# Row sums of squared differences: the first load of x split, another tail, and the tile context closed behind the work

## The chip, the cores and the metric

The kernel runs on one core of a Trainium2 chip. The core has a matrix engine (TensorE or PE, not used here), a vector engine (VectorE or DVE), a scalar engine (ScalarE or ACT), GpSimd (POOL) and SyncE (SP), which here only issues transfers. Sixteen DMA engines carry data between the chip's memory (HBM) and the core's own memory of 128 partitions. The metric is the device time of one execution in microseconds (us); lower is better. Before the change the median of three runs is 85.35 us (85.3 to 85.4).

## The reference

Two arrays of 1024 x 4096 float32 numbers; for each row the sum of the squares of the differences:

```python
def reference(x, y, axis):        # axis = -1
    return np.sum((x - y) ** 2, axis=axis).astype(np.float32)
```

Input is 2 x 16.8 MB, output 4 KB.

## The kernel before

Row 8p + r of the input lies on partition p, so a partition holds eight whole rows side by side: 32768 columns of x and as many of y (N in the code). The text calls the group of 128 rows that share an r "row r"; row r covers the columns 4096 r to 4096 (r + 1). A column of one operand is 128 numbers, 512 bytes. In memory each partition's share is one run of 128 KB.

The core's memory holds six rows of each operand (`X` and `Y`, H = 24576 columns). Columns from 24576 on, rows 6 and 7, go into the places of rows 0 and 1 once these are squared.

**Loads.** The lists `xw` and `yw` give the widths of the pieces, all issued by SyncE on one queue in the order of need (`load`, line 106). Widths shrink towards the end, from 16384 columns to 160. The last 160 columns of row 3 (`late`) are left out of their place in y and loaded after everything else; the last 288 columns of row 7 (`last`) come just before them. A transfer sends one packet for each partition, eight on each of the 16 DMA engines, with as many bytes as the piece has in a partition.

**Work.** For each piece of y VectorE waits for its semaphore and for those of x that it needs (`wait_loaded`, line 153), and subtracts in place, cut at row ends (`sub`, line 163). ScalarE waits for the subtraction and squares with a running sum into one number per partition (`square`, line 168). Where a row has one piece, this number is its result; where it has several, they go into `parts`, and VectorE adds them up (`complete`, line 176): row 6 after the piece with j = 4, row 7 after the last piece. The last piece (row 3's end) isn't given to ScalarE: one VectorE instruction squares, sums, and adds row 3's first part (line 199).

**Order.** There is no scheduler. Each engine's instructions run in the order of the code, and semaphores tie the engines together (`diffs`, `acts`, `sums`, `stored`, one for each load). After the square of row 1 SyncE issues all loads of rows 6 and 7 (line 215). When `sums` is complete it issues the store (line 226).

**Start and end.** The framework puts an entry block in front: all engines pass a barrier there. `Program.early` moves the two first loads (of x and of y) ahead of SyncE's part in it. A `TileContext`, when it is closed, adds a drain, two more barriers of all engines with a clearing of its semaphores between them (there are none to clear where it holds none), and a branch to its block. The kernel closes it at once (line 18), so these barriers stand at the start. The work follows, and at the end GpSimd waits for the store and clears the kernel's semaphores (line 45 and 46).

Of the kernel before, what the change touches and what calls it, by code (L numbers as in the profile page):

```python
# [8 lines left out]
class Program:  # L9
# [4 lines left out]


    def __init__(self, nc, tc):
        self.nc = nc
        tc.close()
        tc.compile()  # L19
        self.here = nc.cur_bb.bb.instructions  # L20
        self.entry = nc.main_func.blocks[0].instructions
        self.before = len(self.here)
        self.sems = []

    def semaphore(self, name):
        self.sems.append(self.nc.alloc_semaphore(name))
        return self.sems[-1]

    def early(self, engine):

        taken = self.here[self.before :]
        del self.here[self.before :]
        where = next(
            n
            for n, i in enumerate(self.entry)
            if i.engine == engine and str(i.opcode) == "Drain"
        )
        self.entry[where:where] = taken

    def close(self, sem, value):  # L40

        self.nc.gpsimd.wait_ge(sem, value)
        self.nc.clear_and_free_semaphores(self.sems)


def kernel(tc, x, y, axis, out):
    nc = tc.nc  # L50
    P = nc.NUM_PARTITIONS
    F32 = mybir.dt.float32
    Square = mybir.ActivationFunctionType.Square
    mult, add = mybir.AluOpType.mult, mybir.AluOpType.add

    B, D = x.shape
    R = B // P
    N = R * D


    xv = x.rearrange("(p r) d -> p (r d)", p=P)
    yv = y.rearrange("(p r) d -> p (r d)", p=P)
    ov = out.rearrange("(p r) -> p r", p=P)


    H = 6 * D
    X = nc.alloc_sbuf_tensor("X", [P, H], F32).ap()
    Y = nc.alloc_sbuf_tensor("Y", [P, H], F32).ap()
    results = nc.alloc_sbuf_tensor("results", [P, R], F32).ap()

    xw = [16384, 8192, 5568, 1824, 512, 288]
    yw = [16224, 8192, 2656, 2912, 928, 896, 512]
    late, last = 160, 288
    LATE = 3
    cut = (LATE + 1) * D - late
    assert sum(xw) == N and sum(yw) == N - late - last
    xs, c = [], 0
    for w in xw:  # L80
        xs.append((c, c + w))
        c += w
    ys, c = [], 0
    for w in yw:
        ys.append((c, c + w))
        c += w
        if c == cut:
            c += late
    ys += [(N - last, N), (cut, cut + late)]

    prog = Program(nc, tc)
    diffs = prog.semaphore("diffs")
    acts = prog.semaphore("acts")
    sums = prog.semaphore("sums")
    stored = prog.semaphore("stored")
    n = dict(diffs=0, acts=0, sums=0)

    def home(c0, c1):
        h0 = c0 % H
        return slice(h0, h0 + c1 - c0)  # L100


    landed_x, landed_y = [], []
    freed = []

    def load(landed, src, dst, name, c0, c1):
        sem = prog.semaphore("%s%d" % (name, len(landed)))
        nc.sync.dma_start(out=dst[:, home(c0, c1)], in_=src[:, c0:c1]).then_inc(sem, 16)  # L108
        landed.append(((c0, c1), sem))

    order = []
    have = 0
    for c0, c1 in ys:
        while have < c1:
            order.append((landed_x, xv, X, "x") + xs[len([o for o in order if o[3] == "x"])])
            have = order[-1][5]
        order.append((landed_y, yv, Y, "y", c0, c1))

    todo = list(order)
    for _ in range(2):  # L120
        load(*todo.pop(0))
    prog.early(mybir.EngineType.SP)
    while todo and todo[0][5] <= H:
        load(*todo.pop(0))


    row_parts = [[] for _ in range(R)]
    for c0, c1 in ys:
        while c0 < c1:
            e = min(c1, (c0 // D + 1) * D)  # L130
            row_parts[c0 // D].append((c0, e))
            c0 = e
    parts, where = None, {}
    total = sum(len(p) for p in row_parts if len(p) > 1)
    parts = nc.alloc_sbuf_tensor("parts", [P, total], F32).ap()
    k = 0
    for r, p in enumerate(row_parts):
        for piece in p:
            where[piece] = parts[:, k : k + 1] if len(p) > 1 else results[:, r : r + 1]
            k += len(p) > 1  # L140
    first = {}
    k = 0
    for r, p in enumerate(row_parts):
        if len(p) > 1:
            first[r] = k
            k += len(p)

    def parts_of(r, m):
        return parts[:, first[r] : first[r] + m]

    seen_x = [0]

    def wait_loaded(c1, ysem):

        waits = []
        while seen_x[0] < len(xs) and xs[seen_x[0]][0] < c1:
            waits.append(seen_x[0])
            seen_x[0] += 1
        nc.vector.wait_ge(ysem, 16)
        for k in waits:  # L160
            nc.vector.wait_ge(landed_x[k][1], 16)

    def sub(c0, c1):
        a = X[:, home(c0, c1)]
        nc.vector.tensor_sub(out=a, in0=a, in1=Y[:, home(c0, c1)]).then_inc(diffs, 1)  # L165
        n["diffs"] += 1

    def square(c0, c1, acc):
        a = X[:, home(c0, c1)]
        nc.scalar.wait_ge(diffs, n["diffs"])  # L170
        nc.scalar.activation(out=a, in_=a, func=Square, accum_out=acc).then_inc(acts, 1)  # L171
        n["acts"] += 1

    squared = {}

    def complete(r):
        nc.vector.wait_ge(acts, squared[row_parts[r][-1]])
        nc.vector.tensor_reduce(  # L178
            out=results[:, r : r + 1],
            in_=parts_of(r, len(row_parts[r])),  # L180
            axis=mybir.AxisListType.X,
            op=add,
        ).then_inc(sums, 1)
        n["sums"] += 1

    for j, (c0, c1) in enumerate(ys):
        final = j == len(ys) - 1
        wait_loaded(c1, landed_y[j][1])
        pieces = []
        while c0 < c1:  # L190
            e = min(c1, (c0 // D + 1) * D)
            pieces.append((c0, e))
            c0 = e
        for piece in pieces:
            sub(*piece)
            r = piece[0] // D
            if final:
                nc.vector.wait_ge(diffs, n["diffs"])
                nc.vector.tensor_tensor_reduce(  # L199
                    out=Y[:, home(*piece)],  # L200
                    in0=X[:, home(*piece)],
                    in1=X[:, home(*piece)],
                    scale=1.0,
                    scalar=parts_of(r, 1),
                    op0=mult,
                    op1=add,
                    accum_out=results[:, r : r + 1],
                ).then_inc(sums, 1)
                n["sums"] += 1
                continue  # L210
            square(*piece, where[piece])
            squared[piece] = n["acts"]
            if r in (0, 1):

                nc.sync.wait_ge(acts, n["acts"])  # L215
                while todo and todo[0][5] <= H + (r + 1) * D:
                    load(*todo.pop(0))
                if r == 1:
                    while todo:
                        load(*todo.pop(0))  # L220
        if j == 4:
            complete(6)
    complete(7)

    nc.sync.wait_ge(sums, n["sums"])
    nc.sync.dma_start(out=ov, in_=results).then_inc(stored, 16)
    prog.close(stored, 16)


# [33 lines left out]
```

## Time and profile before

| | |
|---|---|
| the profiled execution | 85.35 us |
| its span, from the first instruction to the last | 83.5 us |
| what lies around the span | 1.84 us |
| VectorE busy | 36.3 us (44%) |
| ScalarE busy | 31.7 us (38%) |
| data moved | 33.56 MB in 2304 packets on one queue |
| share of the 16 DMA engines that the packets took | 94.7% of the span |
| store, from issue to landing | 1.4 us |

Times in rows are in us from the span's start. Each row of a group or of the timeline names the engine, the line of the kernel, the operation, the tensors written and read, and the count. A name with a q behind it (SPq, POOLq) is the engine's sequencer, which handles semaphores, drains, and the issue of transfers; this isn't counted as busy time. The idle time in brackets is that of the engine just before, with what ended it. Matters of less than a microsecond are decided by the records of single instructions, packets and semaphores in the same trace.

### The profile page before, as it was taken

What the parts mean: (1) busy time and instruction counts of PE and PEld (TensorE: products, weight loads), DVE (VectorE), ACT (ScalarE), POOL (GpSimd) and SP (SyncE); (2) the same over time, 40 slices, a digit from 0 to 9 for tenths busy, and PEclk for the clock granted to TensorE, in tenths of its full rate; (3) what the DMA queues carried; (4) which work ended last, traced back from release to release, by engine and by line L of the source; (5) the groups of instructions that cost most, each with busy time, mean ns of one, the idle gap of its engine ahead of it and who ended that gap; (6) DMA issues with size and microseconds to landing.
All of it is one profiled execution on the core that took longest, in us unless ns stands there. A gap on an engine that the chain in (4) does not pass through costs nothing.

```text
span 83.5 us, 109 instructions
## 1 busy us (share of the span) xinstructions
DVE 36.3 (44%) x18; ACT 31.7 (38%) x27; POOL 0.2 (0%) x4
## 2 busy tenths in 40 slices
DVE  0000000000000000000299999999099995979980
ACT  0500000000000000000001979697970897989990
POOL 0000000000000000000000000000000000000000
DMA  9389999956999999589989998997999899999920
GB/s 471 157 377 502 502 502 502 471 251 283 497 497 497 497 497 404 218 373 497 439 377 439 487 439 345 487 487 330 423 437 437 378 443 427 423 407 410 394 66 2
DMA packets 2305, 33.56 MB, mean 402 GB/s; under 512 B 385, under 2 KB 769, under 8 KB 1409
## 3 DMA queue, kind: packets, MB, share of 16 engines
q1 hardware_dynamic: 2304, 33.56, 94.7%
q14 instruction: 1, 0.00, 0.0%
HBM read 33.55 MB, written 0.00 MB: 402 GB/s over the span
## 4 chain that ended last, share of the span: by engine, by line
DMA 68%; ACT 14%; DVE 14%; SPq 1%; issue 0%
DMA Y<-in_y_dram 68%; ACT X L171 14%; DVE X L165 14%; SPq L108 1%; DVE results L178 0%; SPq L215 0%
## 5 line engine op out<-in xcount | busy, mean ns | idle before, releaser
L165 DVE TENSOR_TENSOR X<-X,Y 128x4096 f32<-128x4096 f32 (+9 forms) x14 | 35.8, 2593 | 45.2 <-DMA Y<-in_y_dram 45.1
L171 ACT ACTIVATE X<-X 128x4096 f32<-128x4096 f32 (+8 forms) x13 | 29.7, 2287 | 48.0 <-DVE X L165 48.0
L171 ACT ACTIVATION_READ_ACCUMULATOR X<-X 128x1 f32 x13 | 2.4, 186 | 0.0
L171 ACT ACT_TABLE_LOAD x1 | 1.3, 1283 | 1.9 <-PEq L19 1.9
L178 DVE TENSOR_REDUCE results<-parts 128x1 f32<-128x2 f32 (+1 forms) x2 | 0.3, 152 | 0.2 <-ACT X L171 0.2
L199 DVE CUSTOM_DVE_ANT_0 Y<-X,parts 128x160 f32<-128x160 f32 x1 | 0.4, 385 | 0.0
L244 POOL MEMSET const-bfloat16-1.0<- 128x1 bf16 x1 | 0.1, 101 | 0.0
L244 POOL MEMSET const-uint8-127<- 128x1 uint8 x1 | 0.1, 101 | 0.0
L244 POOL MEMSET const-float32-0.0<- 128x1 f32 x1 | 0.1, 98 | 0.2 <-issue 0.2
L244 POOL MEMSET const-float32-1.0<- 128x1 f32 x1 | 0.1, 98 | 0.0
L199 DVE DVE_READ_ACCUMULATOR2_ANT results<- 128x1 f32 x1 | 0.1, 83 | 0.0
## 6 DMA issues: line engine op xcount, KB each, us to landing
Y<-in_y_dram SPq DMA_DIRECT2D x1, 8112.0 KB, 40.7
X<-in_x_dram SPq DMA_DIRECT2D x1, 4096.0 KB, 48.9
Y<-in_y_dram SPq DMA_DIRECT2D x1, 4096.0 KB, 58.3
X<-in_x_dram SPq DMA_DIRECT2D x1, 2784.0 KB, 13.4
Y<-in_y_dram SPq DMA_DIRECT2D x1, 1456.0 KB, 19.2
Y<-in_y_dram SPq DMA_DIRECT2D x1, 1328.0 KB, 16.2
X<-in_x_dram SPq DMA_DIRECT2D x1, 912.0 KB, 21.0
Y<-in_y_dram SPq DMA_DIRECT2D x1, 464.0 KB, 21.6
```

The lines of the kernel that those rows point to most:

```text
L108: nc.sync.dma_start(out=dst[:, home(c0, c1)], in_=src[:, c0:c1]).then_inc(sem, 16)
L165: nc.vector.tensor_sub(out=a, in0=a, in1=Y[:, home(c0, c1)]).then_inc(diffs, 1)
L171: nc.scalar.activation(out=a, in_=a, func=Square, accum_out=acc).then_inc(acts, 1)
L178: nc.vector.tensor_reduce(out=results[:, r : r + 1], in_=parts_of(r, len(row_parts[r])), axis=mybir.AxisListType.X, op=add,).then_inc(sums, 1)
L199: nc.vector.tensor_tensor_reduce(out=Y[:, home(*piece)], in0=X[:, home(*piece)], in1=X[:, home(*piece)], scale=1.0, scalar=parts_of(r, 1), ...
L244: nc = _bacc.Bacc("TRN2", target_bir_lowering=False, num_devices=1)
```

## The change

1. **Loads.** The first load of x is cut by columns into 512 (2 KB for each partition) and 15872. It is these two that are issued ahead of the entry barrier; the first load of y (15648) comes behind it. The later widths change too: 8 loads of x and 8 of y, in place of 6 and 9.
2. **Tail.** Row 3's end is 736 columns and comes last but one; row 7's end of 352 columns comes last. ScalarE squares row 3's end and adds row 3's two parts with one Identity activation (part b plus part a as its bias), into `results`. Row 7's first parts are added by VectorE into `head`, and the instruction that squares, sums and adds now works on row 7's 352 last columns with `head`. Row 6 is added up after the fourth piece from the end.
3. **Refill.** The loads into the places of row 0 can now be issued once row 0 is squared, those into row 1's after row 1, as the new widths end within row 6 and row 7 so that the code's test (`todo[0][5] <= H + (r + 1) * D`) lets the first two go.
4. **Start and end.** `tc.close()` and `tc.compile()` are no longer called at the start. The kernel's instructions are written outside the context's hook and put into the entry block, in front of its branch. The context is closed by the launch code, behind the work: SyncE waits for the store and branches, then come the context's drain, a barrier, GpSimd's clearing, and a second barrier. The semaphores are the context's own now.

```diff
     def __init__(self, nc, tc):
-        self.nc = nc
-        tc.close()
-        tc.compile()
+        self.nc, self.hook = nc, tc.instruction_hook
         self.here = nc.cur_bb.bb.instructions
         self.entry = nc.main_func.blocks[0].instructions
+        nc.remove_inst_callback(self.hook)
+        self.lower, nc._always_lower_symbolic_ap = nc._always_lower_symbolic_ap, False
         self.before = len(self.here)
...
-    def close(self, sem, value):
-        self.nc.gpsimd.wait_ge(sem, value)
-        self.nc.clear_and_free_semaphores(self.sems)
+    def close(self):
+        self._put(
+            next(
+                n for n, i in enumerate(self.entry) if str(i.opcode) == "UnconditionalBranch"
+            )
+        )
...
-    xw = [16384, 8192, 5568, 1824, 512, 288]
-    yw = [16224, 8192, 2656, 2912, 928, 896, 512]
-    late, last = 160, 288
+    xw = [512, 15872, 8192, 3072, 2688, 1312, 768, 352]
+    yw = [15648, 8192, 3072, 2688, 1312, 768]
+    late, last = 736, 352
...
-    ys += [(N - last, N), (cut, cut + late)]
+    ys += [(cut, cut + late), (N - last, N)]
...
             if final:
+                nc.vector.wait_ge(acts, squared[row_parts[r][-2]])
+                nc.vector.tensor_reduce(
+                    out=head, in_=parts_of(r, len(row_parts[r]) - 1), axis=mybir.AxisListType.X, op=add
+                ).then_inc(sums, 1)
+                n["sums"] += 1
+                nc.vector.wait_ge(sums, n["sums"])
                 nc.vector.wait_ge(diffs, n["diffs"])
                 nc.vector.tensor_tensor_reduce(
...
-                    scalar=parts_of(r, 1),
+                    scalar=head,
...
+            if tail:
+                a, b = parts_of(r, 1), parts[:, first[r] + 1 : first[r] + 2]
+                nc.scalar.wait_ge(acts, n["acts"])
+                nc.scalar.activation(
+                    out=results[:, r : r + 1], in_=b, func=Identity, bias=a
+                ).then_inc(acts, 1)
+                n["acts"] += 1
...
-        if j == 4:
-            complete(6)
-    complete(7)
+        if j == len(ys) - 4:
...
     nc.sync.wait_ge(sums, n["sums"])
+    nc.sync.wait_ge(acts, n["acts"])
     nc.sync.dma_start(out=ov, in_=results).then_inc(stored, 16)
-    prog.close(stored, 16)
+    nc.sync.wait_ge(stored, 16)
+    prog.close()
```

## The prediction

> **What bounds the kernel now.** I read the table of stages first, then the chain of work that ended last, then both ends of the span. The stages, each with busy time of the vector and scalar engine, granted clock, share of the DMA engines and GB/s:
>
> ```profile
> 0.00:2.00 2.00, 0.00 (x0) 0.09 (x1) 0.20 (x4) 1.00 1.51 492
> 2.00:4.50 2.50, 0.00 (x0) 1.20 (x1) 0.00 (x0) 1.00 0.79 341
> 40.00:60.00 20.00, 17.27 (x4) 12.69 (x7) 0.00 (x0) 1.00 1.01 434
> 80.20:83.50 3.30, 1.29 (x6) 1.40 (x6) 0.00 (x0) 1.00 0.02 1
> ```
>
> The DMA engines are full from just after the start to 80.2 us, at 434 GB/s where nothing starts or ends. 33.55 MB at that rate is 77.3 us of the span of 83.5. The bytes don't change, so only what lies before the stream, after it, or in its gaps can. (The shares over 1 in the first row come of packets being booked where they start.)
>
> The chain from 70.4 us on shows what follows the stream:
>
> ```profile
> 70.37 2.94 DVE X L165
> 73.31 0.02 issue
> 73.33 8.28 ACT X L171 x14
> 81.61 0.02 issue
> 81.64 0.16 DVE results L178
> ```
>
> ScalarE squares without a gap for 8.28 us, so at the end it, not the stream, is what the last sum (L178) waits for. The last load was issued at 65.07 and took 15.4 us, so it landed at 80.47; the sum ended at 81.79. 1.32 us of compute is thus exposed.
>
> The end, in order of time, and the two instructions behind the store:
>
> ```profile
> 79.56 1.43 DVE L165 TENSOR_TENSOR X<-X,Y 128x512 f32<-128x512 f32 x3 [0.18 <-DMA Y<-in_y_dram]
> 81.02 0.39 DVE L199 CUSTOM_DVE_ANT_0 Y<-X,parts 128x160 f32<-128x160 f32 x1
> 81.33 0.08 DVE L199 DVE_READ_ACCUMULATOR2_ANT results<- 128x1 f32 x1
> 81.82 0.35 SPq L226 DMA_DIRECT2D out_dram<-results  x1
> ...
> L46 POOLq DRAIN  x1: 88/88/88, 83.3 to 83.3; - x1
> L46 POOLq EVENT_SEMAPHORE_RANGE_CLEAR  x1: 138/138/138, 83.4 to 83.4; - x1
> ```
>
> The store is issued at 81.82, lands 1.41 us later (83.23), and GpSimd alone drains (83.257) and clears semaphores (83.374 to 83.512). Nothing else stands between the store and the end: 0.28 us.
>
> **The sum's base.** The profiled execution took 85.35 us: span 83.5 and 1.84 around it. The median of the runs is also 85.35, so sums against the one are sums against the other.
>
> **1. The exit.** The tile context now closes after the work. SyncE waits for the store, branches, drains twice; then come a round of all five engines (gather, release), GpSimd's drain and clear, and a second round. Before, two such rounds stood at the start (line 19), beside the transfers already in flight, at no cost:
>
> ```profile
> L19 POOLq EVENT_SEMAPHORE  x4: 17/17/17, 1.4 to 1.8; - x4
> L19 SPq DRAIN  x3: 7/7/7, 1.2 to 1.6; - x3
> L19 PEldq EVENT_SEMAPHORE  x2: 51/51/51, 1.5 to 1.8; - x2
> ```
>
> Their instruction records give the price. Release seen by SyncE at 1.176, taken in 0.017, branch, drain at 1.247: 0.05 for the branch. Drain 1.247, second drain 1.305, gather 1.384, release 1.462, GpSimd's next drain 1.543. So from the landing at 83.23: SyncE's wait 0.03, branch 0.05, then 0.30 to GpSimd's drain, which comes at 83.61 instead of 83.257: +0.35. The drain and clear cost what they did. Behind the clear, the second round: GpSimd's drain and gather about 0.1, gather to release 0.078, release to PE's event 0.054, and its 0.051: 0.28. Together **+0.63**, where line 19's two rounds (1.215 to 1.894) took 0.68. Low bound 0.35, if the end that is timed is GpSimd's clear and the last round falls into the 1.84; high 0.9, if the late branch costs two tenths more than the early one. I take 0.63, made of rows for the same instructions.
>
> The Trainium skill (Runtime: NRT & Kernel Launch, Instruction fetch mechanics) says that a taken branch can force a fetch where its target lies outside the fetched window; it gives no price. The row above has 0.05 for the branch at the start, where this may not have occurred; a fetch would come on top of the sum.
>
> **2. One load more.** 15 loads become 16, with the same bytes. A queued load costs the stream little beyond its bytes: the two 4096 KB loads landed 9.7 us apart, where 434 GB/s gives 9.66; the last eight loads of before (2704 KB) landed over 6.64 us (73.83 to 80.47), where the rate gives 6.38, so 0.03 each. A line through the packet records (51 ns for 1152 B, 2418 for 65536) leaves 9 ns beside the bytes, and a load has eight data packets an engine and one for its semaphore: 0.08. Bounds 0.03 and 0.08; I take **+0.06**, as the landings and the records differ, so the last landing moves to 80.53.
>
> The Trainium skill (DMA: Bandwidth & Descriptors, Rules for kernel authors, and its fit of 2.0 us plus bytes for one DMA) asks for 1 MiB or more per load, and this one is 256 KB. By that fit an exposed load more would cost 2.0 us, and my sum would end near 87.9. The trace's 0.03 for loads queued back to back is the nearer row, so the sum goes by that.
>
> **3. The first packets.** The DMA view of the first 5 us, in 40 slices of 0.125 us, bytes booked where a packet starts:
>
> ```profile
> GB/s 0 0 0 0 0 0 0 1049 3146 3670 0 0 0 0 0 0 524 0 0 0 0 0 0 0 0 0 0 0 0 0 0 524 1049 524 2621 1573 1573 0 524 0
> ```
>
> 524 is one packet of 64 KB. Fifteen engines start between 1.0 and 1.25, the sixteenth at 2.1; second packets start from 3.96 to 4.75. A packet in the stream takes 2.42 us (65536 B at 434/16 GB/s), these 2.78 to 3.54: 0.36 to 1.12 more. The engines then stay about 0.75 us apart to the end, and the last of them sets each landing. If 2 KB packets took all of it away, the stream would end up to 1.1 us earlier (bound −1.1). If it is the time until a first answer comes back, it is paid whatever the packet's size, and nothing changes. If the 63 KB packets behind the short ones pay it again, +0.4 to +1.1. I take **0**: the engine that started at 2.1 took 2.44 us, so the delay belongs to the moment (nothing flows before about 1.5 to 2.3 us), not to a 64 KB packet. Small packets as such are no loss: the 1152-byte loads landed 0.34 us apart, 0.04 per packet, at the full rate. No hole follows: packets come 1.0 us behind an issue, the second x load is issued at about 0.43, so they are there at 1.45 to 1.7, while eight 2 KB packets an engine (0.67 us) on top of the delay last to 2.3 or later.
>
> The first load of y is now issued behind the entry barrier, at about 1.25 instead of 0.43. x keeps the engines busy to about 22 us: hidden; were that cover gone, 0.8. Later issues on SyncE now wait for the first row's square, then the second's (about 49 and 53 us), with loads in flight to 60 us: hidden too. Behind each wait stand only later loads.
>
> **4. The tail.** Two 352-column loads come last, 352 x 512 B at 434 GB/s = 0.42 and 0.03 over, so row 3's 736 columns land at 80.53 − 0.90 = 79.63. DVE's subtract costs 1.04 ns a column and 0.15 fixed (4421 ns for 4096, 319 for 160); the next starts 0.08 before one's end. 736 columns: 79.66, free at 80.50, so it just keeps up. 352: 80.56, free at 81.00. The new sum of row 7's first parts (147 ns by L178) 81.00 to 81.15. L199 on 352 instead of 160 columns: 0.385 + 192 x 1.04 ns = 0.585, from 81.18 to 81.77, its read 0.01 past that: 81.78. This is the place of 81.79 before.
>
> ScalarE loses its last squares (512 and 288) to DVE. 768 columns: from 79.75, 0.83; 736 columns: from 80.61, 0.80, its read to 81.50; then the new Identity on 128x1, which waits for that read: about 0.2 (the fixed part of 187 ns in the squares' rows) and a wait of 0.03: 81.7 to 81.8. Both engines end together, so the store goes at 81.81, **−0.01** against 81.82, with +0.06 inside. Bounds ±0.15, the gap between two neighbouring instructions there.
>
> **Sum.** 85.35 + 0.63 (exit) − 0.01 (tail, with the load more) + 0 (start) = **86.0 us**.
>
> **Rivals.**
> - *The start gains.* Short first packets free the engines of the 0.36 to 1.12 us. For it: the delay is in the rows, and the latest engine sets the end. Against: the engine that started at 2.1. The slowest engine's 1.1 gives 84.9, the middle one's 0.8 gives 85.2. It is faster from a gain of 0.8 on. Chance 0.11. A half gain (0.45 to 0.8) ends at 85.2 to 85.5, 0.08.
> - *The exit is not timed whole.* The second round falls into what lies around the span and the first takes the 0.35: 85.6 to 85.7, and 85.35 if all is absorbed. The whole absorption 0.04, the rest is within the range of the forecast.
> - *The start is paid twice.* The long packets start cold behind the short ones: 86.4 to 87.1. Against: x's loads run on without a gap where one packet follows another. Chance 0.12.
> - *The change doesn't do what it says:* 512 columns may not go as 2 KB packets. Nothing else would move then; still 86.0.
>
> **How the numbers follow.** My forecast with its own range of 85.6 to 86.3 has 0.65. Measured runs of before spread over 0.1 us, so 0.2% (0.17 us) is about what can be told. Faster: the start's gain, 0.11. Same: half gain and absorption, 0.12. Slower: 0.77. The range 85.2 to 86.5 leaves out most of the full gain and the larger part of the double start.
>
> **What would show it.** Right: range clear ending near 83.9 and events of all engines to 84.15; first L199-type sum ending near 81.8; the second x load's landing near 22.1. The start's rival: that landing at 21.0 to 21.5 with all later ones earlier alike. A double start: at 22.5 or later. My forecast is wrong if the exit costs under 0.35, or if every landing moves by more than 0.3.

## The result

The changed kernel takes 85.98 us (85.78 to 86.09), the one before 85.32 us on the same chip: a ratio of 1.0076, with a 95% interval of 1.0053 to 1.0099. It is slower by 0.45 to 0.84 us, and the forecast was 86.0. The sum hit the number more exactly than its terms did: one of them had the wrong sign.

The profiled execution took 86.09 us, 84.31 of it span and 1.78 around it. The stages of it, in the columns of before (stretch, length, VectorE, ScalarE, GpSimd, clock, share of the DMA engines, GB/s):

```profile
0.00:2.00 2.00, 0.00 (x0) 0.74 (x1) 0.20 (x4) 1.00 0.78 247
2.00:4.50 2.50, 0.00 (x0) 0.54 (x1) 0.00 (x0) 1.00 0.83 314
40.00:60.00 20.00, 16.78 (x5) 13.87 (x7) 0.00 (x0) 1.00 0.98 423
80.20:84.30 4.10, 1.53 (x5) 1.62 (x5) 0.00 (x0) 1.00 0.02 1
```

The stream still ends soon after 80.2 us, but 4.1 us stand behind that instead of 3.3. (Packets are booked where they start, and one 64 KB packet for each of the 16 engines is 52 GB/s of a stretch of 20 us; so 423 against 434 says nothing.) The chain that ended last, from there back:

```profile
73.71 3.04 DVE X L172 x2
76.75 0.02 issue
76.77 1.68 ACT X L178 x2
78.46 0.02 issue
78.47 3.06 ACT X L178 x6
81.53 0.02 issue
81.55 0.29 ACT results L219
```

ScalarE is no longer busy without a gap from 73.3 on: the chain stays with VectorE until 76.75 and is ScalarE's from 76.77 to the end. What it ends in is new: the Identity of line 219. The end in order of time:

```profile
80.99 0.15 DVE L196 TENSOR_REDUCE head<-parts 128x1 f32<-128x3 f32 x1
81.22 0.58 DVE L202 CUSTOM_DVE_ANT_0 Y<-X,head 128x352 f32<-128x352 f32 x1
81.34 0.19 ACT L178 ACTIVATION_READ_ACCUMULATOR X<-X 128x1 f32 x1
81.55 0.29 ACT L219 ACTIVATE results<-parts 128x1 f32<-128x1 f32 x1
81.73 0.08 DVE L202 DVE_READ_ACCUMULATOR2_ANT results<- 128x1 f32 x1
81.94 0.35 SPq L245 DMA_DIRECT2D out_dram<-results  x1
```

The last load landed at 80.52 (80.47 before), the store was issued at 81.94 (81.82) and landed at 83.35 (83.23). What stands behind that, from the view of the line that closes the context (operation, count, shortest/median/longest in ns, first and last start):

```profile
L278 POOLq EVENT_SEMAPHORE  x4: 17/17/17, 83.6 to 84.2; - x4
...
L278 SPq DRAIN  x3: 7/7/7, 83.5 to 83.8; - x3
...
L278 PEldq EVENT_SEMAPHORE  x2: 51/51/51, 83.7 to 84.3; - x2
L278 SPq COMPARE_BRANCH  x1: 33/33/33, 83.4 to 83.4; - x1
L278 POOLq EVENT_SEMAPHORE_RANGE_CLEAR  x1: 139/139/139, 83.9 to 83.9; - x1
```

From the store's landing to the end of the span it is 0.96 us, and it was 0.28. So of the 0.80 us by which the span grew, 0.68 lie behind the store's landing, 0.07 between the last load's landing and the store's issue (1.42 against 1.35), and 0.05 in the stream. 0.06 less lies around the span.

### The profile page after: what moved, and what is told of

It is laid out like the page before. It is cut to its first block, busy times and chain, and to the rows that moved or that the text cites. A ratio compares the mean times of both kernels' runs of the same rounds, so it can differ in the third digit from the quotient of the medians.

```text
span 84.3 us, 111 instructions
## 1 busy us (share of the span) xinstructions
DVE 36.3 (43%) x17; ACT 31.6 (38%) x26; POOL 0.2 (0%) x4
## 4 chain that ended last, share of the span: by engine, by line
DMA 71%; DVE 14%; ACT 10%; SPq 0%; issue 0%
DMA Y<-in_y_dram 71%; DVE X L172 14%; ACT X L178 10%; SPq L114 0%; ACT results L219 0%
## 5 line engine op out<-in xcount | busy, mean ns | idle before, releaser
L172 DVE TENSOR_TENSOR X<-X,Y 128x4096 f32<-128x4096 f32 (+8 forms) x13 | 35.6, 2781 | 45.4 <-DMA Y<-in_y_dram 45.4
L178 ACT ACTIVATE X<-X 128x4096 f32<-128x4096 f32 (+7 forms) x12 | 29.4, 2449 | 48.9 <-DVE X L172 48.9
L202 DVE CUSTOM_DVE_ANT_0 Y<-X,head 128x352 f32<-128x352 f32 x1 | 0.6, 583 | 0.1
## 6 DMA issues: line engine op xcount, KB each, us to landing
X<-in_x_dram SPq DMA_DIRECT2D x1, 7936.0 KB, 21.5
```

Source lines behind the costliest of these rows:

```text
L202: nc.vector.tensor_tensor_reduce(out=Y[:, home(*piece)], in0=X[:, home(*piece)], in1=X[:, home(*piece)], scale=1.0, scalar=head, op0=mult, ...
```

## Experiments

All are against the kernel before on the same chip. "Tail" is the time from the last load's landing to the store's issue, "exit" from the store's landing to the end of the span, "around" the execution's time less its span; these three are from one profiled execution each, the ratio from all runs. What was expected of each run stands with it below.

| run | time, us | before, us | ratio (95%) | tail | exit | around |
|---|---|---|---|---|---|---|
| before | 85.32 | | 1 | 1.35 | 0.28 | 1.84 |
| the change | 85.98 | 85.32 | 1.0076 (1.0053 to 1.0099) | 1.42 | 0.96 | 1.78 |
| split_only | 85.15 | 85.22 | 0.9994 (0.9982 to 1.0007) | 1.35 | 0.28 | 1.84 |
| late_close_only | 85.90 | 85.22 | 1.0075 (1.0055 to 1.0094) | 1.35 | 0.97 | 1.78 |
| after_early_close | 85.35 | 85.22 | 1.0012 (1.0000 to 1.0024) | 1.42 | 0.28 | 1.84 |
| tail_only | 85.44 | 85.22 | 1.0020 (1.0004 to 1.0036) | 1.43 | 0.28 | 1.84 |
| split_64 | 85.61 | 85.23 | 1.0043 (1.0029 to 1.0056) | 1.34 | 0.28 | 1.84 |
| sync_clears | 84.59 | 85.23 | 0.9920 (0.9907 to 0.9933) | 1.35 | 0.08 | 1.32 |
| clear_beside_store | 84.48 | 85.23 | 0.9909 (0.9894 to 0.9924) | 1.35 | 0.03 | 1.32 |
| combined | 84.33 | 85.23 | 0.9892 (0.9876 to 0.9909) | 1.00 | 0.03 | 1.33 |
| act_clears | 84.75 | 85.19 | 0.9942 (0.9928 to 0.9957) | 1.35 | 0.14 | 1.48 |
| tail_one_wait | 85.33 | 85.19 | 1.0021 (1.0007 to 1.0034) | 1.37 | 0.27 | 1.83 |
| after_no_split | 86.08 | 85.19 | 1.0102 (1.0085 to 1.0118) | 1.42 | 0.97 | 1.79 |
| combined_no_split | 84.23 | 85.19 | 0.9887 (0.9870 to 0.9904) | 0.97 | 0.03 | 1.33 |

### One part of the change at a time

`late_close_only` has the kernel before with the new `Program`, its semaphores from the context, and this end:

```diff
-    prog.close(stored, 16)
+    nc.sync.wait_ge(stored, 16)
+    prog.close()
```

> The kernel before, with only the closing changed: its work stands in the entry block, SyncE waits for the store, and the context closes behind it. My theory: the whole loss is here, 0.96 instead of 0.28 us from the store's landing to the end of the span, so 85.32 + 0.68 = 86.0. Rival (the last barrier falls into what lies around the span, and the tail makes the difference): 85.3 to 85.7.

Measured: 85.90, 0.1 below my theory's 86.0, which started from 85.32 where before is 85.22 on this chip. The exit is 0.97, the tail is that of before, and the loss of 0.64 us (0.75%) is as large as that of the whole change. `after_early_close` is the reverse, the changed kernel with the old closing:

```diff
-        self.nc, self.hook = nc, tc.instruction_hook
+        self.nc = nc
+        tc.close()
+        tc.compile()
...
-    nc.sync.wait_ge(stored, 16)
-    prog.close()
+    prog.close(stored, 16)
```

> The changed kernel with its context closed at once and GpSimd waiting for the store, as before; split and tail stay. My theory: 85.98 - 0.68 = 85.3, with the store still issued near 81.9 because of the new tail. Rival (split and tail cost the difference): 85.8 or more.

Measured: 85.35, within 0.24% of before. Putting the closing back takes the loss away. The tail stays at 1.42.

`split_only` has this edit alone, in the kernel before; with it SyncE issues y's first load behind the barriers:

```diff
-    xw = [16384, 8192, 5568, 1824, 512, 288]
+    xw = [512, 15872, 8192, 5568, 1824, 512, 288]
```

> The kernel before, with only its first load of x cut into 512 and 15872 columns (these two ahead of the entry barrier, y's first load behind it). My theory: the delay of the first packets is paid whatever their size, and a queued load costs 0.03 to 0.08: landings of the second x load near 22.0, time 85.3 to 85.4. Rival (short first packets take the delay away): landings and time earlier by 0.3 or more, 85.0 or less.

Measured: no difference (0.9982 to 1.0007). The second x load landed at 21.86. In the four profiles with x's first load cut at 512 columns this landing lies at 21.70 to 21.93, and in the nine with it whole the first load's lies at 21.76 to 22.00: nothing like the 21.0 to 21.5 that a gain at the start would need. `tail_only` is the kernel before with the new widths (and with them the refill in two steps) and the tail's code of the change, without split, closed at once. Of its edit, the widths and the order of the last pieces:

```diff
-    xw = [16384, 8192, 5568, 1824, 512, 288]
-    yw = [16224, 8192, 2656, 2912, 928, 896, 512]
-    late, last = 160, 288
+    xw = [16384, 8192, 3072, 2688, 1312, 768, 352]
+    yw = [15648, 8192, 3072, 2688, 1312, 768]
+    late, last = 736, 352
...
-    ys += [(N - last, N), (cut, cut + late)]
+    ys += [(cut, cut + late), (N - last, N)]
```

> The kernel before with only the new widths and the new tail: no split of the first load, context closed at once. My theory: the store is issued 0.1 later than before (the Identity took 0.29 and not 0.2, and SyncE passes two waits), so 85.4. Against the run with the split it tells what the split brings: equal within 0.1 by my theory, 0.3 or more slower than it by the rival that the start gains.

Measured: 85.44, slower by 0.03 to 0.31 us. The trace holds 0.08 of it in the tail; last landings alone range from 80.25 to 80.70 over the runs with the same bytes, so one profile can't tell where more would lie. Against after_early_close, which differs from it by the split alone, it is 0.09 us slower, and the two intervals overlap (1.0000 to 1.0024 and 1.0004 to 1.0036): equal within 0.1, as expected.

The three parts alone add up to −0.05 + 0.17 + 0.64 = 0.76 us, where the whole change has 0.45 to 0.84: no effect between the parts is needed. The refill has no run of its own. The last of this kind, the changed kernel with x's first load whole:

```diff
-    xw = [512, 15872, 8192, 3072, 2688, 1312, 768, 352]
+    xw = [16384, 8192, 3072, 2688, 1312, 768, 352]
```

> The changed kernel with its first load of x whole (16384 columns), and with it y's first load ahead of the entry barrier again. My theory (the split is worth no more than 0.1 either way): 85.9 to 86.1, and 1.85 past GpSimd's last instruction. Rival (the split gives back part of what the exit takes): 86.2 or more.

Measured: 86.08, inside my range, but before was 85.19 on this chip, so the ratio of 1.0102 lies above the change's 1.0076. The two intervals overlap. A gain of the split of some 0.2 us in this kernel is thus neither shown nor excluded by the times. The two profiled executions took 86.09 us each, with the last landings at 80.52 and 80.49, and in the three other pairs (split_only and before, after_early_close and tail_only, combined and combined_no_split) no difference can be told.

### Shorter first packets still

```diff
-    xw = [16384, 8192, 5568, 1824, 512, 288]
+    xw = [64, 16320, 8192, 5568, 1824, 512, 288]
```

> The kernel before with its first load of x cut into 64 columns (256 bytes a packet) and 16320. My theory (the delay of the first packets belongs to the moment, not to their size): the second x load lands between 21.8 and 22.1 as with 512 columns and as without a cut, time 85.2 within 0.15. Rival (the shorter the first packets, the less delay): landing earlier than with 512 columns by 0.2 or more, time 85.0 or less.

Measured: 0.38 us slower, so the rival is wrong, and my "within 0.15" too. The DMA view of the first 5 us in slices of 0.125 us (bytes booked where a packet starts):

```profile
GB/s 0 0 0 0 0 0 0 2 90 92 60 3152 1567 2611 1044 0 0 0 0 0 0 0 0 0 0 0 0 0 0 0 0 0 0 0 0 522 2089 1567 1567 2611
```

The 256-byte packets are through by 1.45 us, and the long ones behind them start at once, but by the packet records they take 2.97 to 3.29 us where 2.41 is the rule, and end at 4.46 to 4.98. The delay has gone over to the second load's packets. So it isn't a matter of the moment alone, as the forecast had it: the long packet that started last here, at 1.83, took 3.10, where before the one that started at 2.10 took 2.44, and one that started at 1.78 in act_clears took 2.49.

This also shows where the 0.38 lies. The median of the 16 engines is through with its first long packet at 4.75, where it is 4.25 to 4.41 in the nine profiles with a whole first load; the 1.8 KB more that it has moved are worth 0.07. The lag stays: x's second load landed at 22.15 (21.76 to 22.00 with the first load whole), the last load at 80.66. Why the first long packets are slow is not shown.

The same view of split_only, with 2 KB packets:

```profile
GB/s 0 0 0 0 0 0 0 33 164 213 180 295 279 885 836 2720 2065 1540 508 508 0 0 0 0 0 0 0 0 0 0 0 0 0 0 0 1016 2032 1016 508 1524
```

The short packets trickle until 2.2 us, the long ones start between 1.72 and 2.41 and end at 4.47 to 5.14. Before, the first 64 KB were through at 3.96 to 4.75; the 14 KB more that an engine has moved here are worth 0.53 us at 2.42 us for 64 KB, which gives 4.49 to 5.28. So the slowest engine is 0.14 ahead in this pair of profiles, less than the 0.45 by which landings differ between runs of the same bytes. The median engine, less the 0.53, is through at 4.15 to 4.24 in the four profiles with this cut, against 4.25 to 4.41 with a whole load. That is a gain of some 0.1, against which stands one load more (0.03 to 0.08 by the forecast's estimate); nothing of it is clear in the times.

### Who ends the program

Up to here the time around the span was 1.84 us wherever GpSimd's clear came last. Two runs take GpSimd off the end. `sync_clears`:

```diff
-        self.nc.gpsimd.wait_ge(sem, value)
-        self.nc.clear_and_free_semaphores(self.sems)
+        self.nc.sync.wait_ge(sem, value)
+        ids = sorted(s.num for s in self.sems)
+        self.nc.sync.sem_clear(range(ids[0], ids[-1] + 1))
```

> The kernel before, with SyncE and not GpSimd waiting for the store and clearing the semaphores, without the drain between. My theory (what stands behind the store's landing is timed in full): the clear starts about 0.05 behind the landing instead of 0.15, so 0.1 less: 85.1. Rival (a late SyncE costs as much in what lies around the span): no change, 85.2.

`clear_beside_store`, where the store's semaphore is also allocated first:

```diff
-        self.nc.gpsimd.wait_ge(sem, value)
-        self.nc.clear_and_free_semaphores(self.sems)
+        issued = self.nc.alloc_semaphore("issued")
+        self.nc.sync.sem_inc(issued, 1)
+        self.nc.gpsimd.wait_ge(issued, 1)
+        self.nc.clear_and_free_semaphores([s for s in self.sems if s is not sem] + [issued])
+        self.nc.sync.wait_ge(sem, value).then_inc(sem, -value)
```

> The kernel before, with GpSimd clearing all semaphores but the store's while the store is under way, and SyncE waiting for the store and taking its 16 off. My theory: 0.28 us behind the landing become about 0.05, so 85.22 - 0.23 = 85.0. Rival (what is taken off the end of the span comes back in what lies around it): 85.2.

Measured: 84.59 and 84.48, each 0.5 us below what my theory had. The exit shrank by 0.20, where 0.1 was expected (SyncE's clear is also the shorter one), and by 0.25, where 0.23 was. Lines of the clears, first of sync_clears, then of clear_beside_store:

```profile
L47 SPq EVENT_SEMAPHORE_RANGE_CLEAR  x1: 64/64/64, 83.2 to 83.2; - x1
```

```profile
L48 POOLq EVENT_SEMAPHORE_RANGE_CLEAR  x1: 138/138/138, 82.6 to 82.6; - x1
```

The other 0.52 us came from what lies around the span: 1.32 instead of 1.84. I had taken this for a constant. Both together are 0.72 and 0.77 (measured 0.64 and 0.75). To see whether it is GpSimd or SyncE that is special, the same with ScalarE:

```diff
-        self.nc.sync.wait_ge(sem, value)
+        self.nc.scalar.wait_ge(sem, value)
         ids = sorted(s.num for s in self.sems)
-        self.nc.sync.sem_clear(range(ids[0], ids[-1] + 1))
+        self.nc.scalar.sem_clear(range(ids[0], ids[-1] + 1))
```

> The kernel before, with ScalarE in place of GpSimd waiting for the store and clearing the semaphores. In the profiled executions so far the time was 1.84 to 1.87 us past GpSimd's last instruction where GpSimd ended last, and 1.32 past the end of the span where SyncE did. My theory (GpSimd's last half microsecond is GpSimd's own, any other engine may end later without it): about 1.3 past the end of the span, 84.6. Rival (the end of SyncE alone is cheap): 1.84 past it, 85.1.

```profile
L47 ACTq EVENT_SEMAPHORE_RANGE_CLEAR  x1: 114/114/114, 83.0 to 83.0; - x1
```

Measured: 84.75, with 1.48 around the span. So both my 1.3 and the rival's 1.84 are missed: it is 1.84 behind GpSimd, 1.48 behind ScalarE, 1.32 behind SyncE. The value for ScalarE is from one profile, those for the two others from four and more. That the end costs more on GpSimd is shown; what runs there isn't seen in the trace.

With this the changed kernel's own 1.78 can be read. Its span ends with PE's event at 84.31, but GpSimd's last instruction ends at 84.22, and the time is 1.87 past that; in late_close_only and after_no_split it is 1.87 and 1.88. So of the last 0.09 us of the second barrier, most seems to lie beside GpSimd's own end, and 0.03 to count (1.87 against 1.84). That is argued: no run has PE end last without GpSimd just before it, so PE's own end may as well set the time.

### The tail

`tail_one_wait`, in tail_only:

```diff
-                    out=results[:, r : r + 1], in_=b, func=Identity, bias=a
-                ).then_inc(acts, 1)
+                    out=results[:, r : r + 1], in_=b, func=Identity, bias=a
+                ).then_inc(both, 1)
...
                     accum_out=results[:, r : r + 1],
-                ).then_inc(sums, 1)
+                ).then_inc(both, 1)
...
-    nc.sync.wait_ge(sums, n["sums"])
-    nc.sync.wait_ge(acts, n["acts"])
+    nc.sync.wait_ge(both, 2)
```

> The run with only the new tail, but the Identity and the last sum post to one semaphore, so that SyncE passes one wait ahead of the store. My theory (two terms that I had not priced make the tail slower: the Identity's 0.29 and the second wait's 0.06): the store is issued about 0.03 behind the later of the two instead of 0.1, so 0.06 less than with two waits: 85.3 to 85.4. Rival (the order of the last pieces costs the time): as before this edit, 85.4 to 85.5, with the store as far behind the last sum.

Ends of tail_only, then of tail_one_wait:

```profile
81.60 0.29 ACT L214 ACTIVATE results<-parts 128x1 f32<-128x1 f32 x1
81.76 0.08 DVE L197 DVE_READ_ACCUMULATOR2_ANT results<- 128x1 f32 x1
81.98 0.35 SPq L240 DMA_DIRECT2D out_dram<-results  x1
```

```profile
81.44 0.29 ACT L214 ACTIVATE results<-parts 128x1 f32<-128x1 f32 x1
81.60 0.08 DVE L198 DVE_READ_ACCUMULATOR2_ANT results<- 128x1 f32 x1
81.76 0.35 SPq L238 DMA_DIRECT2D out_dram<-results  x1
```

The Identity's end (81.89 and 81.73) is the later one in both. The store follows 0.09 behind it with two waits and 0.03 with one: the second wait costs 0.06, as expected. In the time nothing of it is seen: 85.33 lies in my range, but the ratio is 1.0021 where tail_only has 1.0020. So the second wait is 0.06 of the 0.08 by which tail_only's tail is longer in the trace; what else stands behind its 0.17 us in the time, such as the order of the last pieces, stays open.

`combined` is clear_beside_store with the split and these widths, in the tail of before:

```diff
-    xw = [16384, 8192, 5568, 1824, 512, 288]
-    yw = [16224, 8192, 2656, 2912, 928, 896, 512]
-    late, last = 160, 288
+    xw = [512, 15872, 8192, 3424, 2208, 992, 704, 384, 320, 160]
+    yw = [16192, 8192, 3424, 2208, 992, 704, 384, 320]
+    late, last = 192, 160
```

> The kernel before with the clearing beside the store, the first load of x cut into 512 and 15872 columns, and new widths for rows 6 and 7 (3424, 2208, 992, 704, 384, 320, 160, and 192 columns of row 3's end last), chosen so that ScalarE is not behind at the end. My theory: 0.23 from the exit, 0.05 from the cut, and up to 0.25 from the tail, where the row 7 sum then waits for the stream and not for ScalarE: 84.7 to 84.9. Rival (the additional loads, 0.03 to 0.08 each, eat the tail's gain): 84.95 or more.

Its chain at the end:

```profile
71.66 8.43 DMA Y<-in_y_dram
80.09 0.02 issue
80.11 0.63 DVE X L168 x2
80.74 0.02 issue
80.76 0.42 DVE Y L202
81.18 0.01 DVE results L202
81.19 0.13 DVE results L181
```

Measured: 84.33, 0.9 us below before and below my range, which didn't have the 0.52 around the span. Here the chain goes straight from the stream to VectorE, and ScalarE isn't in it, so the tail is 1.00 and not 1.35. In the time it is 0.15 us below clear_beside_store, with overlapping intervals (0.9876 to 0.9909 and 0.9894 to 0.9924): that the shorter tail gains anything isn't clear of the noise, and whether the five loads more eat part of its 0.35, as the rival has it, isn't settled. Without the split:

```diff
-    xw = [512, 15872, 8192, 3424, 2208, 992, 704, 384, 320, 160]
+    xw = [16384, 8192, 3424, 2208, 992, 704, 384, 320, 160]
```

> The combined version with its first load of x whole. My theory: no difference beyond 0.1, so 84.3 to 84.4. Rival (the split matters where the stream sets the end): 84.5 or more.

Measured: 84.23, not to be told from the other. This simpler one has the lowest time of the study, 0.96 to 1.3% below the kernel before; combined and clear_beside_store can't be told from it.

## Why the prediction was right, and where not

**The exit (+0.63).** Right, as the cause and nearly in size: late_close_only alone is 0.64 slower, after_early_close isn't slower by more than 0.24%. In the span the exit grew by 0.68. The part that was too small is the branch: 0.05 from the start's rows, but by the instruction records SyncE's branch begins at 83.367 and the drain behind it at 83.519, 0.15. In late_close_only it is 0.15 as well. The sum's high bound had allowed for this. From there on the rounds came close to line 19's rows: 0.25 to GpSimd's drain where the sum had 0.30, and 0.29 for the second round where it had 0.28. So the clear ended at 84.02 and the last event at 84.31, where the signs on record were 83.9 and 84.15. A fetch behind a taken branch, which the Trainium skill (Runtime: NRT & Kernel Launch, Instruction fetch mechanics) holds possible, isn't seen here: the DMA view of neither run has a packet of the instruction queue (q14) in the span, though the view of before shows that this queue is recorded. Why the late branch takes 0.10 more stays open. Against it, 0.06 of the last round isn't in the time, as the rival of an untimed exit would have it, by a tenth of its size.

**What lies around the span.** The base took 1.84 as given. For this change it was 0.06 too much (1.78); it isn't a constant, as 1.32 behind SyncE shows.

**One load more (+0.06).** The last load landed at 80.52, forecast 80.53. As the landings range over 0.45 us from run to run, this agreement shows only that nothing like the 2.0 us of the fit is paid: combined carries five loads more than before, and its last landing was 80.35. The Trainium skill (DMA: Bandwidth & Descriptors, Anatomy of one DMA — SWDGE (gpsimd) path) gives that fit for transfers issued by GpSimd. The loads here are issued by SyncE on a hardware queue and queued back to back, and the prediction doesn't say that the fit isn't given for such.

**The first packets (0).** The result was right for this change: split_only has 0.9994, and the bounds (−1.1 and +1.1) were far too wide. The second x load landed at 21.93, near the 22.1 on record as a sign. The reason given, that nothing flows before about 1.5 to 2.3 us, was not right: with 256-byte packets all of the first load was through at 1.45, and the long packets behind it were slow all the same. In split_64 the long packets paid again behind the short ones, as one of the rivals had it, and the run was 0.38 us slower; with 2 KB packets the time shows nothing of the kind.

**The tail (−0.01).** This step failed. It let the store go at 81.81; it went at 81.94, with the last landing as forecast, but 1.42 behind it instead of the sum's 1.28 (1.35 before). Three terms were too small. The Identity on 128x1, at "about 0.2 (the fixed part of 187 ns in the squares' rows)", took 0.294. SyncE's second wait, 0.06, wasn't in the sum at all, though the code shows it. And between the new sum of row 7's first parts and line 202, which passes two waits, lie 0.08 and not 0.03; this one wasn't on the path, as ScalarE ended last. The subtracts and squares themselves came within 0.02 (line 202 at 0.583 for 0.585). So "both engines end together" was right (81.81 and 81.85), but later than said by 0.03 and some 0.1, and with 0.09 and not 0.03 on top.

**The rivals.** Neither a gain nor a double payment at the start occurred, and the 512 columns did go as packets of 2 KB (128 of them in the records). The 0.13 by which the tail was too short and the 0.05 by which the exit was were met by the 0.06 around the span and by the spread between executions (85.78 to 86.09): the median's 85.98 against 86.0 owes something to luck.

## What to carry to other kernels

Where a stream of loads fills the whole span, look at what lies behind its last landing. In this kernel the barriers, drains and clear there cost 0.64 us for 0.68 of span, while at the start, beside the stream, such barriers cost nothing that could be measured (after_early_close). Clear the semaphores beside the last store, let only a wait of SyncE follow it (0.75 us less here), and count each semaphore wait of the engine that issues the store (0.06 in the trace). The delay at the start of the stream wasn't removed by cutting the first load, at 512 or at 64 columns.

## What was not expected

- The time around the span depends on who ends last: 1.84 us behind GpSimd, 1.48 behind ScalarE, 1.32 behind SyncE. In this kernel that half microsecond is nearly as much as the whole change.
- The same range clear takes 138 ns on GpSimd, 114 on ScalarE and 64 on SyncE.
- An Identity on one column takes 294 ns, where squares of 4096 columns have a fixed part of 187.
- With 256-byte packets ahead of the stream the kernel is 0.29 to 0.56% slower, with 2 KB packets no slower that could be measured.
